# Gate and up products of the feed-forward with the tokens standing still, their product turned by TensorE transposes

## The chip, the core and the metric

One core of one Trainium2 chip runs the kernel. The metric is the device time of one execution in microseconds (us), here the median of three runs. TensorE multiplies a stationary operand of 128 x 128 numbers, which it loads first (the profile's PEld rows), with up to 512 columns that stream past it (the PE rows), and adds the results in PSUM. VectorE (DVE) and ScalarE (ACT) read PSUM and prepare operands; transfers are issued by SyncE (SP).

## The reference, cut to what matters

A decoder trunk of two layers on 256 tokens of width 2048: a layer with dilated attention, then one with latent attention, each followed by a SwiGLU feed-forward of hidden width 5632. All of it is float32.

```python
def swiglu(xn, w_gu, w_down):                      # xn (256, 2048), w_gu (2048, 2 * 5632), w_down (5632, 2048)
    g, u = jnp.split(xn @ w_gu, 2, axis=-1)
    return (jax.nn.silu(g) * u) @ w_down

for layer in range(DEPTH):                         # DEPTH = 2
    ...
    h = h + swiglu(rms_norm(h, ffn_norm_g[layer]), ffn_w_gu[layer], ffn_w_down[layer])
return rms_norm(h, final_norm_g)
```

## The kernel before

**Precision.** Every float32 operand of the large products is split into two float32r parts, hi + lo. A product is made of three: hi by hi, hi by lo, lo by hi. Activations lie transposed, features on partitions: `xT[:, k, 0:256]` holds the hi part of feature tile k for 256 tokens, `xT[:, k, 256:512]` the lo part.

**Weights.** `WeightStream` walks a fixed list of units of 1 MB (2048 float32 per partition). SP loads a unit into one of four `raw` buffers; ACT makes `hi` by two casts (L141), DVE makes `lo` by two subtractions (L142), each half a unit. `hi` and `lo` have three buffers each, so the split of a unit can start when TensorE has finished the unit three before it. The stream has 176 units for gate and up (two layers of 88), each 8 feature tiles by 256 weight columns, and 88 units for the down product, each 4 feature tiles by 512 columns.

**Two forms of product.** `product` takes an accumulator of two PSUM banks (two such accumulators exist), and for each unit calls one of these:

- `w_stationary` (gate, up, and attention's queries and keys): 128 weight columns stand still, the tokens stream. For each feature tile and each of two blocks of 128 weight columns there are two matmuls: the hi weights against 512 columns [hi | lo of the tokens] (L398), and the lo weights against 256 columns (L402). The result has features on partitions, with two halves that are still to be added.
- `x_stationary` (attention's values, the output projection, down): 128 tokens stand still, 512 weight columns stream. For each feature tile and each of two token tiles there are three matmuls of 512 columns (L419, L420, L421). The result has tokens on partitions.

**Feed-forward.** `ffn` works through the 44 hidden tiles of 128 in three parts of 16, 16 and 12. In a part it computes gate and up for two hidden tiles at a time (two units for each): ACT copies one half of the accumulator (L438), DVE adds the halves (L439), DVE multiplies gate by the tokens' rms scale `R` (L389; `across` made R with a small matmul, L383), ACT applies Silu (L604), DVE multiplies gate by up (L606), and `put_split` writes hi and lo of the hidden tiles into `hT` (ACT L326, DVE L327). Then the part's down product runs, four times 512 output columns, with `hT` standing still; `add` puts each result into the residual `h` (L610).

**Transposes.** `transposed` turns token-major tiles into features on partitions: four TensorE transposes of 128 x 128 into a PSUM bank (L351), then `put_split` from the bank. Two banks, eight transposes, are one call for 512 columns. Before the change it serves the normed operands (`h`, `xt`) and the latent vectors (`cc`).

**Order.** Each engine runs its own list in order. `Later` puts a piece of work behind the matmuls of a following unit: `later.put(1, f)` runs f after the matmuls of the next unit, so TensorE has a unit to do while the other engines prepare what f reads.

Of the kernel before, what the change touches and what calls it, by code (L numbers as in the profile page):

```python
# [36 lines left out]
# Weight tiles between a head's projections and its scores, its values.  # L37
# [9 lines left out]
def shape_constants():  # L47
    """Identity, attention masks and rotary tables: functions of the shapes alone."""
    c = np.zeros((P, C_END), np.float32)
    c[:, C_ID:C_ID + P] = np.eye(P, dtype=np.float32)  # L50

    def allowed(q, k, window, dil):
        dist = q - k
        return (dist >= 0) & (dist <= window) & (dist % dil == 0)

    def put(at, blocks):
        m = np.concatenate([allowed(q[:, None], k[None, :], w, d) for q, k, w, d in blocks], axis=1)
        c[:, at:at + m.shape[1]] = np.where(m, np.float32(0.0), np.float32(NEG))

    # Layer A keeps the even tokens in tile 0 and the odd ones in tile 1.  # L60
    i = np.arange(P)
    par = (2 * i, 2 * i + 1)
    order = np.concatenate(par)
    put(C_M0, [(q, order, *A_GROUPS[0]) for q in par])
    put(C_M1, [(q, q, *A_GROUPS[1]) for q in par])
    put(C_M2, [(q, q, *A_GROUPS[2]) for q in par])
    put(C_MB, [(i, i, S, 1), (i + P, np.arange(S), S, 1)])

    def angles(dim):
        f = np.float32(THETA) ** (-np.arange(0, dim, 2, dtype=np.float32) / np.float32(dim))  # L70
        a = np.arange(S, dtype=np.float32)[:, None] * f.astype(np.float32)[None, :]
        return np.cos(a).T.astype(np.float32), np.sin(a).T.astype(np.float32)

    ca, sa = (t[:, order] for t in angles(A_ROT))
    c[:A_ROT, C_CA:C_CA + S] = np.concatenate([ca, ca], axis=0)
    c[:A_ROT, C_SA:C_SA + S] = np.concatenate([-sa, sa], axis=0)
    cb, sb = angles(ROPE)
    c[:, C_CB:C_CB + S] = np.concatenate([cb, cb, cb, cb], axis=0)
    c[:, C_SB:C_SB + S] = np.concatenate([-sb, sb, -sb, sb], axis=0)
    return c  # L80


class WeightStream:
    """Weight tiles in the order of use: loads run ahead, and each float32 tile is split
    exactly into two float32r parts (hi + lo) ahead of the matmuls. form: "dup" writes the
    columns of every k twice, "heads" puts the rotary columns of a pair of heads side by side."""
# [17 lines left out]
    def pieces(self, raw, hi, lo, form, gain):  # L104
        """(source, hi, lo, gain) of every split operation."""
# [7 lines left out]
        elif gain is None:  # L113
            flat = lambda t: t.rearrange("p k c -> p (k c)")  # noqa: E731
            n = nk // 2
            for ks in (slice(0, n), slice(n, nk)):
                yield flat(raw[:, ks]), flat(hi[:, ks]), flat(lo[:, ks]), None
        else:
            for k in range(nk):
                src, dst = raw[:, k, :], [hi[:, k, :], lo[:, k, :]]  # L120
                if form == "dup":
                    src = src.unsqueeze(1).broadcast_to([P, 2, ncol])
                    dst = [t.rearrange("p (o c) -> p o c", o=2) for t in dst]
                yield src, dst[0], dst[1], gain[:, k:k + 1]

    def split(self, upto):
        nc = self.nc
        while self.n_split < min(upto, len(self.units)):
# [8 lines left out]
            view = lambda t: t[:, :nk * ncol].rearrange("p (k c) -> p k c", c=ncol)  # noqa: E731  # L137
# [23 lines left out]
class Later:  # L161
    """Work put behind the matmuls of the following weight tiles, so that TensorE has those to do
    while the other engines prepare its operands."""
# [16 lines left out]
def kernel(ctx, tc, consts, x, attn_norm_g, ffn_norm_g, a_w_qkv, a_w_o, kv_norm_g,  # L180
# [23 lines left out]
    # TensorE's clock rises after some microseconds of work: have it up when the data is here.  # L204
# [10 lines left out]
    def gain_cols(vec, name):  # L215
        """vec [n * P] -> [P, n]: rows of P, to be turned by a transpose."""
# [19 lines left out]
    def load_rest():  # L236
        """The constants and gains that the first products don't need."""
# [41 lines left out]
    def units_ffn(layer):  # L279
        for k0, n in FFN_PARTS:  # L280
            for j in range(k0, k0 + n, 2):
                for base in (0, FF):
                    for k in range(0, KD, 8):
                        add_unit(ffn_w_gu[layer], k, 8, base + j * P, 256)
            for c in range(0, D, 512):
                for k in range(k0, k0 + n, 4):
                    add_unit(ffn_w_down[layer], k, 4, c, 512)
# [28 lines left out]
    con = lambda at, n, rows=P: cst[:rows, at - P:at - P + n]  # noqa: E731  # L316
# [6 lines left out]
    def put_split(dst_hi, dst_lo, src, scale=None):  # L323
        """dst_hi + dst_lo = src (times a value per partition), exactly."""
# [8 lines left out]
    def squares(src, total, on_vector=False):  # L333
        """total [P, 1] = the sum of squares of src [P, n] along the free axis."""
# [9 lines left out]
    def transposed(srcs, dstT, k0, gain):  # L344
        """srcs: [P tokens, n] by token tile -> dstT[:, k0 + j, hi 0:S | lo S:2S], features on partitions."""
# [16 lines left out]
    def rsqrt_mean(ssq, n, dst):  # L362
        """dst = (ssq / n + eps) ** -0.5."""
# [4 lines left out]
    def token_scale(ssq, name):  # L368
        """rms scale by token from partial sums of squares [P, NT, n]."""
# [6 lines left out]
    def across(r, name):  # L376
        """r [P tokens, NT] -> [P, S], the tokens' values along the free axis of every partition."""
# [13 lines left out]
    def w_stationary(acc, hi, lo, xT, k0, first, last, cols):  # L391
        """acc[:, i, :] += (weights' columns cols(i))^T [xT hi | xT lo], lo parts of weights on xT hi."""
        nk = hi.shape[1]
        for kk in range(nk):
            k = k0 + kk
            for i, sl in enumerate(cols):
                st, sp = first and kk == 0, last and kk == nk - 1
                big_mm = lambda: mm(out=acc[:, i, :], lhsT=sl(hi, kk), rhs=xT[:, k, :],  # noqa: B023,E731  # L398
                                    start=st, stop=sp)  # noqa: B023
# [6 lines left out]
    def col(i, n=P):  # L406
        return lambda t, kk: t[:, kk, i * n:(i + 1) * n]

    def x_stationary(acc, hi, lo, xT, k0, first, last, rhs=None, ncol=512, ts=range(NT)):
        """acc[:, t, :] += (tokens of tile t) @ weights."""  # L410
# [12 lines left out]
    def product(stationary, xT, K, **kw):  # L423
        """xT's K feature tiles with the next weight tiles, into a new accumulator."""
# [10 lines left out]
    def halves(acc, n, dst):  # L435
        """dst [P, n, S] = acc[:, :, :S] + acc[:, :, S:]."""
# [4 lines left out]
    def masked(dst, ps, mk, mx):  # L441
        """dst = ps + mk, mx = its maximum by row."""
# [3 lines left out]
    def softmax(parts, m, scale, nscale):  # L446
        """parts[t] [P queries, keys] masked scores, m [P, NT] their maxima -> probabilities."""
        nb = small.tile([P, NT], F32, tag="sm_nb", name="sm_nb")
        if isinstance(scale, float):
            nc.vector.tensor_scalar(out=nb, in0=m, scalar1=nscale, scalar2=None, op0=ALU.mult)  # L450
            by = lambda t: scale  # noqa: E731
        else:
            nc.vector.tensor_tensor(out=nb, in0=m, in1=nscale, op=ALU.mult)
            by = lambda t: scale[:, t:t + 1]  # noqa: E731
# [10 lines left out]
    def keys_first(blocks):  # L465
        """Transposes of [P, P] blocks of probabilities, side by side."""
# [27 lines left out]
    with tc.tile_pool(name="attn_a", bufs=2) as ap:  # L494

        def rope_a(t):
            sw = ap.tile([A_ROT, 2, S], F32, tag="sw", name="sw", bufs=1)
            nc.vector.stream_shuffle(sw, t[:A_ROT], swap)
            bc = lambda r: r.unsqueeze(1).broadcast_to([A_ROT, 2, S])  # noqa: E731
# [22 lines left out]
        def values_a(head, sm, vs):  # L522
# [11 lines left out]
            back = lambda d: d.rearrange("p (i t) -> p t i", t=NT)  # noqa: E731  # L534
# [38 lines left out]
    def out_projection(acc, oT, gain, name):  # L573
        """h += attention output @ w_o (its first columns in acc); the next normed operand,
        still to be scaled by token, and that scale."""
# [12 lines left out]
    def ffn(xT, rstd, finish):  # L588
        """h += swiglu(xT scaled by token); finish(c, t) when a piece of h is complete."""
        row = {}  # L590
        later.put(1, lambda: row.update(R=across(rstd, "R")))
        with tc.tile_pool(name="ffn", bufs=2) as fp:
            for part, (k0, n) in enumerate(FFN_PARTS):
                last = part == len(FFN_PARTS) - 1
                hT = big_tile([P, 16, 2 * S], F32R, "hT")
                for j in range(0, n, 2):
                    gu = []
                    for which in range(2):
                        acc = product(w_stationary, xT, KD, cols=(col(0), col(1)))
                        t = fp.tile([P, 2, S], F32, tag=f"gu{which}", name=f"gu{which}")  # L600
                        halves(acc, 2, t)
                        if which == 0:
                            times_row(t, row["R"], 2)
                            nc.scalar.activation(out=t, in_=t, func=AF.Silu)  # L604
                        gu.append(t)
                    nc.vector.tensor_tensor(out=gu[1], in0=gu[1], in1=gu[0], op=ALU.mult)  # L606
                    put_split(hT[:, j:j + 2, 0:S], hT[:, j:j + 2, S:2 * S], gu[1])

                def add(acc, c, t):
                    nc.vector.scalar_tensor_tensor(out=chunk(t, c), in0=acc[:, t, :], scalar=rstd[:, t:t + 1],  # L610
                                                   in1=chunk(t, c), op0=ALU.mult, op1=ALU.add)
                    if last:  # noqa: B023
                        finish(c, t)

                for c in range(4):
# [4 lines left out]
                    else:  # the very last columns: one token tile after the other  # L620
# [29 lines left out]
    with tc.tile_pool(name="attn_b", bufs=2) as bp:  # L650

        def rope_b(dst, t):
            """dst(rows) = rotary of t [P = 2 x (32 | 32), S]."""
# [8 lines left out]
        def latent(at, gain, lag):  # L662
            """rms_norm(xT @ (gained weights)) into ccT, transposed and gained."""
# [25 lines left out]
        # Rotary queries of one head of a pair each, zero in the other head's rows.  # L689
# [127 lines left out]
```

## Time and profile before

| what | us |
|---|---|
| median of 3 runs (lowest 2730.53, highest 2733.0) | 2730.87 |
| profiled execution, first to last instruction (its span) | 2728.2 |
| TensorE busy in it | 2715.6 |
| VectorE busy | 1612.6 |
| ScalarE busy | 1204.2 |

The profiled execution's own device time is not among the rows of the profile; its span is 2.7 us under the median of the runs. A matmul's row lasts longer than the time to the next matmul, since matmuls overlap in the array: the cost of one in a stream is the distance of two starts, and the cost of a stage is the distance from its first start to the next stage's first start.

### The profile page before, as it was taken

The numbers are of one execution on the slowest core, as the hardware profiler recorded it, in microseconds if no ns is written. First come the engines' busy times: TensorE is split into PE (matmuls) and PEld (weight loads), VectorE is DVE, ScalarE is ACT, GpSimd is POOL, SyncE is SP. The second block draws the span as 40 slices with busy tenths as digits, with TensorE's granted clock in tenths as the row PEclk, the third lists the DMA queues.
The fourth block names the chain that finished last, engine by engine and source line by source line (L and its number), as shares of the span: only waits on it lengthen the run. The fifth ranks groups of instructions, "written<-read, shape, count | busy, mean of one in ns | idle before, by whom it ended". The sixth has DMA issues, their size and how long they took to land.

```text
span 2728.2 us, 34772 instructions
## 1 busy us (share of the span) xinstructions
PE 2715.6 (100%) x14398; PEld 2323.1 (85%) x14398; DVE 1612.6 (59%) x2240; ACT 1204.2 (44%) x1605; POOL 5.5 (0%) x12
## 2 busy tenths in 40 slices
PE   9999999999999999999999999999999999999998
PEld 7888888888888888888888888888888888888887
DVE  5666576576477555545555555587555555555554
ACT  5344444443434444434443444555444434443443
POOL 0000000000000000000000000000000000000000
PEclk9999999999999999999999999999999999999999
DMA  7545555554554555555555555454555555555553
GB/s 282 182 162 171 181 171 170 185 182 161 182 175 166 201 181 188 187 190 194 188 185 187 185 187 196 140 156 145 174 181 186 194 190 187 187 190 192 185 201 124
DMA packets 389870, 495.91 MB, mean 182 GB/s; under 512 B 9848, under 2 KB 293200, under 8 KB 389200
## 3 DMA queue, kind: packets, MB, share of 16 engines
q1 hardware_dynamic: 389088, 492.63, 54.2%
q8 instruction: 113, 1.85, 0.3%
q10 hardware_dynamic: 624, 1.07, 0.1%
q14 instruction: 45, 0.37, 0.0%
HBM read 491.57 MB, written 2.10 MB: 181 GB/s over the span
## 4 chain that ended last, share of the span: by engine, by line
PE 98%; DVE 0%; issue 0%; ACT 0%; DMA 0%; SPq 0%; POOL 0%; POOLq 0%; DVEq 0%; ACTq 0%
PE acc L398 39%; PE acc L402 20%; PE acc L420 12%; PE acc L421 12%; PE acc L419 12%; PE bank L513 1%; PE bank L470 1%; PE bank L528 1%; PE bank L351 1%; PE bank L532 1%; PE bank L705 0%; PE bank L704 0%; PE bank L715 0%; DMA xt<-in_x_dram 0%; DVE lo L142 0%
## 5 line engine op out<-in xcount | busy, mean ns | idle before, releaser
L142 DVE TENSOR_TENSOR lo<-raw,hi 128x1024 fp32r<-128x1024 f32 (+2 forms) x930 | 1082.4, 1193 | 570.4 <-ACT hi L141 570.1
L141 ACT CAST hi<-raw 128x1024 fp32r<-128x1024 f32 (+2 forms) x930 | 912.7, 1030 | 859.7 <-issue 358.8
L398 PE MATMUL acc<-xT_f,hi 128*128 128x512 f32 x2816 | 987.6, 398 | 0.0
L402 PE MATMUL acc<-xT_f,lo 128*128 128x256 f32 x2816 | 776.9, 281 | 0.0
L398 PEld LDWEIGHTS acc<-xT_f,hi 128*128 128x128 f32 x2816 | 523.8, 188 | 122.7
L398 PE MATMUL acc<-xT_a,hi 128*128 128x512 f32 x1536 | 544.2, 399 | 0.0
L402 PEld LDWEIGHTS acc<-xT_f,lo 128*128 128x128 f32 x2816 | 531.8, 189 | 7.8
L402 PE MATMUL acc<-xT_a,lo 128*128 128x256 f32 x1536 | 423.7, 281 | 0.0
L398 PEld LDWEIGHTS acc<-xT_a,hi 128*128 128x128 f32 x1536 | 286.8, 188 | 63.5
L438 ACT COPY t<-acc 128x512 f32<-128x512 f32 x161 | 92.7, 576 | 502.8 <-PE acc L398 502.8
L402 PEld LDWEIGHTS acc<-xT_a,lo 128*128 128x128 f32 x1536 | 289.5, 188 | 3.7
L419 PE MATMUL acc<-hi,hT 128*128 128x512 f32 x704 | 274.1, 389 | 0.0
L421 PE MATMUL acc<-hi,hT 128*128 128x512 f32 x704 | 273.9, 389 | 0.0
L420 PE MATMUL acc<-lo,hT 128*128 128x512 f32 x704 | 273.9, 389 | 0.0
L439 DVE TENSOR_TENSOR gu<-acc,t 128x512 f32<-128x512 f32 x88 | 60.9, 692 | 244.2 <-ACT t L438 244.2
L421 PEld LDWEIGHTS acc<-hi,hT 128*128 128x128 f32 x704 | 132.1, 188 | 27.5
L420 PEld LDWEIGHTS acc<-lo,hT 128*128 128x128 f32 x704 | 132.1, 188 | 27.3
L419 PEld LDWEIGHTS acc<-hi,hT 128*128 128x128 f32 x704 | 132.2, 188 | 27.2
L420 PE MATMUL acc<-lo,xT_a 128*128 128x512 f32 x384 | 150.3, 391 | 0.8 <-DVE lo L142 0.8
L421 PE MATMUL acc<-hi,xT_a 128*128 128x512 f32 x384 | 151.0, 393 | 0.0
L419 PE MATMUL acc<-hi,xT_a 128*128 128x512 f32 x384 | 150.9, 393 | 0.0
L420 PEld LDWEIGHTS acc<-lo,xT_a 128*128 128x128 f32 x384 | 72.3, 188 | 16.1 <-DVE lo L142 1.5
(169 smaller groups left out, 2080.7 us busy)
## 6 DMA issues: line engine op xcount, KB each, us to landing
raw<-in_ffn_w_gu_dram SPq DMA_DIRECT2D x176, 1024.0 KB, 4.9
raw<-in_a_w_qkv_dram SPq DMA_DIRECT2D x143, 1024.0 KB, 4.9
raw<-in_ffn_w_down_dram SPq DMA_DIRECT2D x88, 1024.0 KB, 4.9
raw<-in_a_w_o_dram SPq DMA_DIRECT2D x16, 1024.0 KB, 4.9
raw<-in_b_w_o_dram SPq DMA_DIRECT2D x16, 1024.0 KB, 4.9
raw<-in_b_w_kv_b_dram SPq DMA_DIRECT2D x8, 1024.0 KB, 5.4
raw<-in_b_w_q_b_dram SPq DMA_DIRECT2D x8, 768.0 KB, 4.6
raw<-in_b_w_q_a_dram SPq DMA_DIRECT2D x4, 1024.0 KB, 5.0
```

The lines of the kernel that those rows point to most:

```text
L141: nc.scalar.copy(out=h, in_=src)
L142: nc.vector.tensor_tensor(out=l, in0=src, in1=h.bitcast(F32), op=ALU.subtract)
L351: nc.tensor.transpose(out=ps[:, jj * S + t * P:jj * S + (t + 1) * P], in_=srcs[t][:, (j + jj) * P:(j + jj + 1) * P], identity=ident)
L398: big_mm = lambda: mm(out=acc[:, i, :], lhsT=sl(hi, kk), rhs=xT[:, k, :], # noqa: B023,E731 start=st, stop=sp) # noqa: B023
L402: mm(out=acc[:, i, 0:S], lhsT=sl(lo, kk), rhs=xT[:, k, 0:S], start=False, stop=False)
L419: mm(out=acc[:, t, :ncol], lhsT=xh, rhs=rhs(hi, kk), start=st, stop=False)
L420: mm(out=acc[:, t, :ncol], lhsT=xh, rhs=rhs(lo, kk), start=False, stop=False)
L421: mm(out=acc[:, t, :ncol], lhsT=xl, rhs=rhs(hi, kk), start=False, stop=sp)
L438: nc.scalar.copy(out=t1[:, :n, :], in_=acc[:, :n, S:2 * S])
L439: nc.vector.tensor_tensor(out=dst, in0=acc[:, :n, 0:S], in1=t1[:, :n, :], op=ALU.add)
L470: nc.tensor.transpose(out=ps[:, i * P:(i + 1) * P], in_=b, identity=ident)
L513: mm(out=ps[:, t * n:(t + 1) * n], lhsT=q[:, hh, qt], rhs=kt[:, hh, ks], start=True, stop=True)
```

## The change

Gate and up use `x_stationary` instead of `w_stationary`. A step is now four hidden tiles (512 columns) instead of two, and a unit of gate and up is 4 feature tiles by 512 columns instead of 8 by 256, of the same 1 MB. ACT applies Silu straight from the accumulator, with the tokens' rms scale as a value per partition, into a new tile `hid` (tokens on partitions); DVE multiplies `hid` by the up accumulator; after the next unit's matmuls `transposed` turns `hid` by eight TensorE transposes and splits it into `hT`. The sum of the halves, the row `R` and its small matmul are gone from the feed-forward. Comments and docstrings were removed as well.

```diff
     def units_ffn(layer):
         for k0, n in FFN_PARTS:
-            for j in range(k0, k0 + n, 2):
+            for j in range(k0, k0 + n, 4):
                 for base in (0, FF):
-                    for k in range(0, KD, 8):
-                        add_unit(ffn_w_gu[layer], k, 8, base + j * P, 256)
+                    for k in range(0, KD, 4):
+                        add_unit(ffn_w_gu[layer], k, 4, base + j * P, 512)
...
     def ffn(xT, rstd, finish):
-        row = {}
-        later.put(1, lambda: row.update(R=across(rstd, "R")))
-        with tc.tile_pool(name="ffn", bufs=2) as fp:
+        with tc.tile_pool(name="ffn", bufs=3) as fp:
             for part, (k0, n) in enumerate(FFN_PARTS):
                 last = part == len(FFN_PARTS) - 1
                 hT = big_tile([P, 16, 2 * S], F32R, "hT")
-                for j in range(0, n, 2):
-                    gu = []
-                    for which in range(2):
-                        acc = product(w_stationary, xT, KD, cols=(col(0), col(1)))
-                        t = fp.tile([P, 2, S], F32, tag=f"gu{which}", name=f"gu{which}")
-                        halves(acc, 2, t)
-                        if which == 0:
-                            times_row(t, row["R"], 2)
-                            nc.scalar.activation(out=t, in_=t, func=AF.Silu)
-                        gu.append(t)
-                    nc.vector.tensor_tensor(out=gu[1], in0=gu[1], in1=gu[0], op=ALU.mult)
-                    put_split(hT[:, j:j + 2, 0:S], hT[:, j:j + 2, S:2 * S], gu[1])
+                for j in range(0, n, 4):
+                    hid = fp.tile([P, NT, 512], F32, tag="hid", name="hid")
+                    acc = product(x_stationary, xT, KD)
+                    for t in range(NT):
+                        nc.scalar.activation(out=hid[:, t, :], in_=acc[:, t, :], func=AF.Silu,
+                                             scale=rstd[:, t:t + 1])
+                    acc = product(x_stationary, xT, KD)
+                    nc.vector.tensor_tensor(out=hid, in0=acc, in1=hid, op=ALU.mult)
+                    later.put(1, lambda j=j, hid=hid, hT=hT:
+                              transposed([hid[:, t, :] for t in range(NT)], hT, j, None))
```

On TensorE, at the start of the first feed-forward (xT_f is its normed operand, h the residual), the order before has pairs of a long and a short matmul, with the transposes of the last piece of h and the matmul for R between them:

```order
4705 L402 MATMUL acc<-xT_f_7145,lo 128x256
4706 L398 MATMUL acc<-xT_f_7145,hi 128x512
4707 L351 MATMUL bank<-ident,h 128x128 x8
4708 L383 MATMUL bank<-diag,ones 128x256
4709 L402 MATMUL acc<-xT_f_7145,lo 128x256
```

On TensorE, after the first unit of the second step, the order of the changed kernel has triples of 512 columns, and the eight transposes of the first step's hid between two of them:

```order
4892 L421 MATMUL acc<-hi,xT_f_7145 128x512
4893 L351 MATMUL bank<-ident,hid 128x128 x8
4894 L419 MATMUL acc<-hi,xT_f_7145 128x512
4895 L420 MATMUL acc<-lo,xT_f_7145 128x512
4896 L421 MATMUL acc<-hi,xT_f_7145 128x512
```

Such a group of eight stands once in each step of four hidden tiles, 22 times in all, always after the 24 matmuls of the unit that follows the step; the group for h stays where it was and the matmul for R is gone.

On VectorE, at the start of a part of the feed-forward before (lo is a half unit of split weights, gu the gate or up tile, t the copied half), one step of two hidden tiles reads:

```order
911 L142 TENSOR_TENSOR lo<-raw,hi 128x1024 x4
912 L439 TENSOR_TENSOR gu_11574<-acc,t_11575 128x512
913 L389 TENSOR_TENSOR gu_11574<-gu_11574,R 128x512
914 L142 TENSOR_TENSOR lo<-raw,hi 128x1024 x4
915 L439 TENSOR_TENSOR gu_11661<-acc,t_11662 128x512
916 L606 TENSOR_TENSOR gu_11661<-gu_11661,gu_11574 128x512
917 L142 TENSOR_TENSOR lo<-raw,hi 128x1024
918 L327 TENSOR_TENSOR hT<-gu_11661,hT 128x2x256
```

On VectorE, at the start of a part in the changed kernel, one step of four hidden tiles reads:

```order
1199 L142 TENSOR_TENSOR lo<-raw,hi 128x1024 x16
1200 L601 TENSOR_TENSOR hid<-acc,hid 128x1024
1201 L142 TENSOR_TENSOR lo<-raw,hi 128x1024 x3
1202 L327 TENSOR_TENSOR hT<-bank,hT 128x2x256 x2
1203 L142 TENSOR_TENSOR lo<-raw,hi 128x1024 x13
```

Three operations that stood between the halves of weights are gone, the multiplication stands alone and waits for the up product, and the writing of hT has moved three half units behind it, where it waits for the transposes and for ACT's casts of them.

## Rows read from the trace of the kernel before

**Rows 1.** The page: the span, the busy times of the engines, and TensorE's granted clock in 40 slices in tenths of full speed.

```profile
span 2728.2 us, 34772 instructions
...
PE 2715.6 (100%) x14398; PEld 2323.1 (85%) x14398; DVE 1612.6 (59%) x2240; ACT 1204.2 (44%) x1605; POOL 5.5 (0%) x12
...
PEclk9999999999999999999999999999999999999999
```

**Rows 2.** The page: the chain of work that ended last, by engine and by line.

```profile
PE 98%; DVE 0%; issue 0%; ACT 0%; DMA 0%; SPq 0%; POOL 0%; POOLq 0%; DVEq 0%; ACTq 0%
PE acc L398 39%; PE acc L402 20%; PE acc L420 12%; PE acc L421 12%; PE acc L419 12%; PE bank L513 1%; PE bank L470 1%; PE bank L528 1%; PE bank L351 1%; PE bank L532 1%; PE bank L705 0%; PE bank L704 0%; PE bank L715 0%; DMA xt<-in_x_dram 0%; DVE lo L142 0%
```

**Rows 3.** Busy time in the six gate and up stages, of the instructions that read or write xT_f alone. Columns: the stretch, its length, then for PE, PEld, DVE and ACT the busy time (and instructions), the granted clock, the DMA engines' busy share, GB/s. The first three stages are layer 0's, the sum is over all six.

```profile
979.90:1161.79 181.89, 180.93 (x1024) 156.83 (x1023) 1.74 (x4) 1.70 (x4) 1.00 0.56 185
1248.83:1429.42 180.59, 180.59 (x1024) 156.77 (x1023) 0.00 (x0) 0.00 (x0) 1.00 0.57 187
1516.46:1651.90 135.44, 135.44 (x768) 117.54 (x767) 0.00 (x0) 0.00 (x0) 1.00 0.56 186
...
sum 995.84, PE 993.92 PEld 862.30 DVE 3.48 ACT 3.40; mean PE 165.65 PEld 143.72 DVE 0.58 ACT 0.57
```

**Rows 4.** The same view of two of the down stages, of the instructions that read or write hT alone. The second is layer 0's last; it holds three groups of eight transposes of h.

```profile
1161.79:1248.83 87.04, 87.04 (x384) 71.88 (x383) 0.68 (x1) 0.62 (x1) 1.00 0.58 194
...
1651.90:1719.90 68.00, 66.11 (x288) 53.65 (x287) 0.68 (x1) 0.62 (x1) 1.00 0.56 186
```

**Rows 5.** TensorE's instructions in order of time where a down stage ends and a gate and up stage begins: start, length, line, operation.

```profile
1248.15 0.39 PE L419 MATMUL acc<-hi,hT 128*128 128x512 f32 x1
1248.38 0.39 PE L420 MATMUL acc<-lo,hT 128*128 128x512 f32 x1
1248.60 0.39 PE L421 MATMUL acc<-hi,hT 128*128 128x512 f32 x1
1248.83 0.39 PE L398 MATMUL acc<-xT_f,hi 128*128 128x512 f32 x1
1249.06 0.28 PE L402 MATMUL acc<-xT_f,lo 128*128 128x256 f32 x1
1249.17 0.40 PE L398 MATMUL acc<-xT_f,hi 128*128 128x512 f32 x1
```

**Rows 6.** The chain that ended last in order of time (start, length, what), its transposes in layer 0's last down stage. Three units of the down product lie from one group to the next.

```profile
1673.82 0.87 PE bank L351 x8
1691.05 0.87 PE bank L351 x8
1708.28 0.87 PE bank L351 x8
```

**Rows 7.** TensorE's instructions in order of time around the first of these groups.

```profile
1673.43 0.39 PE L421 MATMUL acc<-hi,hT 128*128 128x512 f32 x1
1673.66 1.03 PE L351 MATMUL bank<-ident,h 128*128 128x128 f32 x8
1674.45 0.48 PE L419 MATMUL acc<-hi,hT 128*128 128x512 f32 x1
1674.76 0.39 PE L420 MATMUL acc<-lo,hT 128*128 128x512 f32 x1
```

**Rows 8.** The groups of instructions by line and shape: the transposes of h. After the bar: busy time, mean ns of one, idle time before them.

```profile
L351 PE MATMUL bank<-ident,h 128*128 128x128 f32 x96 | 12.4, 272 | 0.0
```

**Rows 9.** The same view: the halves of the weights' split; then the operations that the change removes or that are like those which it adds, on VectorE and ScalarE.

```profile
L142 DVE TENSOR_TENSOR lo<-raw,hi 128x1024 fp32r<-128x1024 f32 x894 | 1062.8, 1218 | 570.4 <-ACT hi L141 570.1
L141 ACT CAST hi<-raw 128x1024 fp32r<-128x1024 f32 x894 | 896.2, 1050 | 854.8 <-issue 358.8 <-PE acc L421 319.6 <-PE acc L398 173.7
...
L439 DVE TENSOR_TENSOR gu<-acc,t 128x512 f32<-128x512 f32 x88 | 60.9, 692 | 244.2 <-ACT t L438 244.2
...
L604 ACT ACTIVATE gu<-gu 128x512 f32<-128x512 f32 x44 | 27.6, 626 | 0.0
...
L544 ACT ACTIVATE v<-acc,rstd 128x512 f32<-128x512 f32 x24 | 15.2, 685 | 42.1 <-PE acc L421 42.1
...
L582 DVE TENSOR_TENSOR h<-acc,h 128x1024 f32<-128x1024 f32 x8 | 9.8, 1225 | 15.8 <-PE acc L421 13.7 <-DMA h<-in_x_dram 2.1
...
L327 DVE TENSOR_TENSOR xT_b<-bank,xT_b 128x512 fp32r<-128x512 f32 x8 | 5.1, 682 | 0.0
...
L326 ACT CAST xT_b<-bank 128x512 fp32r<-128x512 f32 x8 | 4.2, 582 | 0.0
```

**Rows 10.** VectorE's instructions in order of time in a down stage, around the end of one product (in brackets: idle time before, and what ended it).

```profile
1205.51 1.41 DVE L610 SCALAR_TENSOR_TENSOR h<-acc,rstd,h 128x512 f32<-128x512 f32 x2 [2.00 <-PE acc L421]
1206.84 2.35 DVE L142 TENSOR_TENSOR lo<-raw,hi 128x1024 fp32r<-128x1024 f32 x2
1212.03 2.36 DVE L142 TENSOR_TENSOR lo<-raw,hi 128x1024 fp32r<-128x1024 f32 x2 [2.84 <-ACT hi L141]
```

**Rows 11.** The page: DMA issues of the weights of gate and up (8 runs of 1 KB on each partition) and of down (4 runs of 2 KB): count, KB each, us from issue to landing.

```profile
raw<-in_ffn_w_gu_dram SPq DMA_DIRECT2D x176, 1024.0 KB, 4.9
...
raw<-in_ffn_w_down_dram SPq DMA_DIRECT2D x88, 1024.0 KB, 4.9
```

**Rows 12.** TensorE's instructions in order of time at a group of transposes of the latent vectors whose operand came late.

```profile
1769.28 0.44 PE L351 MATMUL bank<-ident,cc 128*128 128x128 f32 x2 [0.51 <-ACT cc L675]
```

## Prediction

> **What bounds the kernel now.** I read the page's busy times and the chain first: TensorE is busy for 2715.6 of 2728.2 us at a granted clock of 1.00, that is at its 2.4 GHz level, and 98% of the chain that ended last is TensorE [rows 1, 2]. No other engine is near: VectorE 59%, ScalarE 44%. So the time moves by what TensorE's own stream gains or loses, and by nothing else unless a new wait appears in it. Next I read the stages that the change touches. The six gate and up stages last 995.84 us together, with 1024 or 768 matmuls on a clock of 1.00; within them TensorE waits only at the start [rows 3]. The down stages show the other form of product, which the change puts in place of the present one [rows 4].
>
> **The price of a unit in the two forms.** A unit is 1 MB of weights in both. With the weights standing still it is 16 pairs, 32 matmuls: the second stage has 32 units in 180.59 us, 5.643 us each, 0.353 us a pair; the third has 24 units in 135.44 us, the same 5.643 [rows 3]. With the tokens standing still it is 4 feature tiles x 2 token tiles x 3 = 24 matmuls of 512 columns: 384 matmuls, 16 units, take 87.04 us, which is 5.440 us a unit and 0.2267 us a matmul [rows 4]; the starts 1248.15, 1248.38, 1248.60 show it directly [rows 5]. The columns streamed are the same, 16 x (512 + 256) = 24 x 512 = 12288. What differs is only how many matmuls they are cut into, and how a short one's weight load fits behind it. So the gain is small: 0.203 us in 5.643, under 4%, where a glance at the rows' durations (0.398 + 0.281 against 3 x 0.389) would promise 14%. Those durations overlap; the distances of the starts don't.
>
> **Sum, part by part.**
> 1. Gate and up: 176 units x 5.440 = 957.44 us. Of what stands in the present stages beside units, the two groups that transpose the last piece of h stay; they cost 2 x 0.907 = 1.81 (next point). So 995.84 becomes 959.25: 36.59 us less. This counts the small matmul for R and its surroundings, too: the first stage is 181.89 - 180.59 = 1.30 us longer than the second, 0.91 of it the transposes of h, 0.39 the matmul for R and what waited there, twice 0.8 us [rows 3].
> 2. The transposes: 22 groups of eight. Layer 0's last down stage has 12 units and three such groups in 68.00 us; 12 x 5.440 = 65.28, so a group costs 2.72 / 3 = 0.907 us [rows 4]. The chain says the same: from 1673.82 to 1691.05 and to 1708.28 it is 17.23 us, against 3 x 5.440 = 16.32 [rows 6]. These are transposes of float32 tiles of the same shape among the same matmuls, so I take 0.907: 22 x 0.907 = 19.95 us more. The bounds are the group's length on the chain, 0.87, and its length in order of time, 1.03 [rows 6, 7]: 19.1 to 22.7 us.
> 3. Net: 36.59 - 19.95 = 16.6 us less.
>
> A rule of the Trainium skill speaks against point 2. Page "TensorE: Matmul & The Clock Gate", Part 4 (PE-mode transpose), gives about 275 ns for a 128 x 128 transpose in one kernel's context; 176 of them would be an estimated 48.4 us, more than the whole gain, and the kernel would come out near 2743. This trace has that number, 272 ns, as the mean length of a transpose's row, yet eight of them take 0.87 us on the chain [rows 6, 8]: the price in a stream is the distance, 0.11 us.
>
> **What has to stay hidden.** Per step of four hidden tiles the other engines get less work, not more: ACT has two Silu from PSUM (like the 685 ns activation from an accumulator) and two casts from a bank (582 ns), DVE one multiplication of 1024 columns (like the 1225 ns one) and two subtractions (682 ns); four additions of halves (692 ns), two Silu (626 ns) and others go [rows 9]. That relief is worth nothing by itself, since TensorE is the bound. Three chains could turn into a wait:
> - *hid before its transposes.* The multiplication is queued behind the halves of weights of a unit that was split before, and the transposes come after one more unit, 5.44 us. In a down stage DVE picks up a finished accumulator at once, after 2.00 us of idleness [rows 10], so hid is there after 1.3 to 1.5 us: about 4 us to spare.
> - *hT before the down product reads it.* The last step's four tiles are read by the third unit (parts of 12) of down, at 2 x 5.44 + 0.91 = 11.8 us; the transposes begin at 5.44. ACT has one half cast in front (1.05), then two casts (1.16), and DVE finishes 0.7 to 1.4 us later: near 9.1 us, 2.7 to spare [rows 9]. In parts of 16 it is a unit more.
> - *Weights.* The split of a unit takes ACT 2.1 and DVE 2.4 us [rows 9] and has two units' time. The Silu pair in front of it adds 1.4, the hT casts 1.2. The loads land in 4.9 us for either shape of run [rows 11], four buffers ahead, and down stages already run at this pace with 194 GB/s [rows 4]. Here, and for the two PSUM accumulators (each free long before the 21.8 us product that reuses it begins), I take zero.
>
> **The rivals.**
> - *A, hid comes late.* If DVE or ACT were behind, TensorE would stop at each of the 22 groups. The one late group in the trace lost 0.51 us, waiting for ACT's cc [rows 12]: 22 x 0.51 = 11.2, and the kernel would be at 2725.5, hardly faster. For it: hid passes through two engines whose lists hold weight work. Against: 4 us of room.
> - *B, slower: each transpose costs its row.* If transposes of hid did not overlap with each other and with the matmuls' loads, each would take 0.272 us [rows 8], 22 x 8 x 0.272 = 47.9 us, and 2730.87 - 36.59 + 47.9 = 2742.2. It decides from 36.59 / 176 = 0.208 us a transpose. Against: 0.113 at the groups measured [rows 4].
> - *C, slower: gate and up gain nothing.* If the stage went by columns alone, or by the arrival of weights at 187 GB/s [rows 3], a unit would stay at 5.643, only 0.8 us would be saved and 20 paid: about 2750. Against: the down stages' 5.440 with the same loads, splits and operand layout [rows 4].
>
> Rival C can also be read in the Trainium skill: the page "TensorE: Matmul & The Clock Gate", section "Back-to-back issue gap", puts a lone matmul's gap at N / 2.4 + 2.5 ns; by it a unit would be an estimated 5.20 us before and 5.18 after, the saving 4 us and the kernel near 2746. The distances measured here, 0.353 a pair and 0.227 a matmul, are both above it and not equally so, which is where the gain lies [rows 3, 4].
>
> **How the numbers follow.** The sum is made on the profiled execution: 2728.2 - 16.6 = 2711.6 us of span. The runs' median lies 2.7 above that span, and nothing outside the stages changes, so 2730.87 - 16.6 = 2714.2. With the bounds of point 2 it is 2713.4 to 2717.0, and the three runs scatter by 2.5 us. Chances: the forecast 0.84, A 0.08, B 0.03, C 0.03; 0.02 for something unseen. The range is 2711 to 2721: the forecast with its bounds and the scatter, stretched towards a partial A (0.3 us lost at each group gives 2720.8). No change is within 0.2% (5.5 us, about what a measurement of this kernel can tell): 2725.4 to 2736.3. A lies on that edge. Faster 0.89, same 0.06, slower 0.05.
>
> **What would show it.** In the changed profile: gate and up stages of 32 units near 174.1 us plus 0.91 for each group in them, matmul starts 0.227 apart, PE rows of L398 and L402 on xT_f gone, 176 transposes of hid with some 20 us on the chain, no idle time before them, a granted clock of 1.00 throughout. Idle time before L351 released by hid would be A; a group much longer than 0.91 would be B; a unit above 5.5 us, C. The forecast is wrong if the triples on xT_f don't keep the pace of those on hT, or if TensorE waits for lo or hT anywhere in these stages.

## The result, and the profile after

| | before | changed |
|---|---|---|
| median of 5 runs, us (lowest to highest) | 2731.51 (2730.53 to 2733.0) | 2713.31 (2712.54 to 2714.91) |
| span of the profiled execution, us | 2728.2 | 2711.5 |

The ratio is 0.9934, with a 95% interval of 0.9922 to 0.9947: 18.2 us faster by the medians, 16.7 by the spans. The forecast was 2714.2 and 2711.6 of span. That the span agrees to 0.1 us is in part luck, since the spans of the five executions run from 2710.8 to 2713.1; what repeats more closely is the length of the stages below.

The page of the changed kernel, as [rows 1]:

```profile
span 2711.5 us, 31961 instructions
...
PE 2698.2 (100%) x13162; PEld 2269.7 (84%) x13162; DVE 1521.5 (56%) x2080; ACT 1162.8 (43%) x1517; POOL 5.5 (0%) x12
...
PEclk9999999999999999999999999999999999999999
```

Its chain by engine and by line, as [rows 2]:

```profile
PE 98%; DVE 0%; issue 0%; ACT 0%; DMA 0%; SPq 0%; POOL 0%; POOLq 0%; DVEq 0%; ACTq 0%
PE acc L420 24%; PE acc L421 24%; PE acc L419 24%; PE acc L398 15%; PE acc L402 7%; PE bank L351 1%; PE bank L513 1%; PE bank L470 1%; PE bank L528 1%; PE bank L532 1%; PE bank L701 0%; PE bank L700 0%; PE bank L711 0%; DMA xt<-in_x_dram 0%; DVE lo L142 0%
```

TensorE is as full as before, in a shorter span. VectorE and ScalarE are relieved of 91 and 41 us of busy time; whether that has a part in the difference is tested below. The gate and up stages, instructions on xT_f alone, as [rows 3]; the first three are layer 0's, the sum is over six:

```profile
979.81:1157.52 177.71, 175.19 (x768) 143.67 (x767) 1.74 (x4) 1.70 (x4) 1.00 0.58 189
1245.47:1422.27 176.80, 174.91 (x768) 143.74 (x767) 0.00 (x0) 0.00 (x0) 1.00 0.58 190
1510.21:1642.59 132.38, 131.12 (x576) 107.78 (x575) 0.00 (x0) 0.00 (x0) 1.00 0.59 191
...
sum 973.78, PE 962.45 PEld 790.36 DVE 3.48 ACT 3.40; mean PE 160.41 PEld 131.73 DVE 0.58 ACT 0.57
```

and the two down stages of [rows 4]:

```profile
1157.52:1245.47 87.95, 87.32 (x384) 71.81 (x383) 1.28 (x2) 1.07 (x2) 1.00 0.60 192
1642.59:1711.49 68.90, 66.39 (x288) 53.58 (x287) 1.28 (x2) 1.07 (x2) 1.00 0.55 184
```

The second gate and up stage holds 32 units and three groups of transposes: 176.80 - 3 x 0.907 = 174.08, 5.440 us a unit. The fourth group of the part stands in the down stage, which is 0.91 us longer than before. Layer 0's whole feed-forward, from its first matmul to the next layer's first (979.81 to 1711.49), takes 731.68 us where it took 740.00 (979.90 to 1719.90): 8.32 us less, and the second layer's loses as much: 16.64 in all. The starts at the border, as [rows 5], show one pace on both sides of it:

```profile
1245.24 0.39 PE L421 MATMUL acc<-hi,hT 128*128 128x512 f32 x1
1245.47 0.39 PE L419 MATMUL acc<-hi,xT_f 128*128 128x512 f32 x1
1245.69 0.39 PE L420 MATMUL acc<-lo,xT_f 128*128 128x512 f32 x1
```

The chain in order of time, its transposes of hid, as [rows 6]: 44.42 and 44.43 us apart, which is 8 units (43.52) and 0.90.

```profile
1029.85 0.87 PE bank L351 x8
1074.27 0.87 PE bank L351 x8
1118.70 0.87 PE bank L351 x8
```

The new groups of instructions, as [rows 8, 9]:

```profile
L327 DVE TENSOR_TENSOR hT<-bank,hT 128x512 fp32r<-128x512 f32 x44 | 28.2, 682 | 0.0
L598 ACT ACTIVATE hid<-acc,rstd 128x512 f32<-128x512 f32 x44 | 27.9, 686 | 68.7 <-PE acc L421 68.7
L601 DVE TENSOR_TENSOR hid<-acc,hid 128x1024 f32<-128x1024 f32 x22 | 26.9, 1224 | 43.9 <-PE acc L421 43.9
L326 ACT CAST hT<-bank 128x512 fp32r<-128x512 f32 x44 | 23.5, 587 | 0.0
L351 PE MATMUL bank<-ident,hid 128*128 128x128 f32 x176 | 22.8, 272 | 0.0
```

The transposes (L351) have no idle time ahead of them. VectorE in order of time at the tightest place, the start of layer 0's last down stage (up ended at 1642.59), to be read beside [rows 10]:

```profile
1642.79 1.23 DVE L601 TENSOR_TENSOR hid<-acc,hid 128x1024 f32<-128x1024 f32 x1 [1.99 <-PE acc L421]
...
1650.62 1.28 DVE L327 TENSOR_TENSOR hT<-bank,hT 128x512 fp32r<-128x512 f32 x2
```

So hid is there 1.4 us after the end of up and hT 9.3 us after it; TensorE needs them at 5.4 and 11.8.

### The profile page after: what moved, and what is told of

Same layout as the page of the kernel before. It is cut to its first block, busy times and chain, and to the rows that moved or that the text cites. A ratio compares the mean times of both kernels' runs of the same rounds, so it can differ in the third digit from the quotient of the medians.

```text
span 2711.5 us, 31961 instructions
## 1 busy us (share of the span) xinstructions
PE 2698.2 (100%) x13162; PEld 2269.7 (84%) x13162; DVE 1521.5 (56%) x2080; ACT 1162.8 (43%) x1517; POOL 5.5 (0%) x12
## 4 chain that ended last, share of the span: by engine, by line
PE 98%; DVE 0%; issue 0%; ACT 0%; DMA 0%; SPq 0%; POOL 0%; POOLq 0%; DVEq 0%; ACTq 0%
PE acc L420 24%; PE acc L421 24%; PE acc L419 24%; PE acc L398 15%; PE acc L402 7%; PE bank L351 1%; PE bank L513 1%; PE bank L470 1%; PE bank L528 1%; PE bank L532 1%; PE bank L701 0%; PE bank L700 0%; PE bank L711 0%; DMA xt<-in_x_dram 0%; DVE lo L142 0%
## 5 line engine op out<-in xcount | busy, mean ns | idle before, releaser
L419 PE MATMUL acc<-hi,xT_f 128*128 128x512 f32 x1408 | 549.3, 390 | 0.0
L421 PE MATMUL acc<-hi,xT_f 128*128 128x512 f32 x1408 | 548.0, 389 | 0.0
L420 PE MATMUL acc<-lo,xT_f 128*128 128x512 f32 x1408 | 547.9, 389 | 0.0
L421 PEld LDWEIGHTS acc<-hi,xT_f 128*128 128x128 f32 x1408 | 264.3, 188 | 55.0
L420 PEld LDWEIGHTS acc<-lo,xT_f 128*128 128x128 f32 x1408 | 264.3, 188 | 54.4
L419 PEld LDWEIGHTS acc<-hi,xT_f 128*128 128x128 f32 x1408 | 264.3, 188 | 54.3
L438 ACT COPY t<-acc 128x512 f32<-128x512 f32 (+1 forms) x73 | 41.0, 561 | 185.7 <-PE acc L398 185.7
```

Source lines behind the costliest of these rows:

```text
L419: mm(out=acc[:, t, :ncol], lhsT=xh, rhs=rhs(hi, kk), start=st, stop=False)
L420: mm(out=acc[:, t, :ncol], lhsT=xh, rhs=rhs(lo, kk), start=False, stop=False)
L421: mm(out=acc[:, t, :ncol], lhsT=xl, rhs=rhs(hi, kk), start=False, stop=sp)
L438: nc.scalar.copy(out=t1[:, :n, :], in_=acc[:, :n, S:2 * S])
```

## The experiments

Since the sum came out, the question was whether its terms are the reasons or only happen to add up. Each time below stands against runs of the kernel before on the same chip (medians of 2729.82 to 2732.62 us). The changed kernel is 18.2 us faster than its own, and what a run gains or loses to it is taken from these two differences.

**Is 0.907 us what a group costs?** Once the transposes were left out, so that hT is split from hid as it lies:

```diff
-                              transposed([hid[:, t, :] for t in range(NT)], hT, j, None))
+                        for i in range(0, 4, 2):
+                            put_split(hT[:, j + i:j + i + 2, 0:S], ..., hid[:, :, i * P:(i + 2) * P])
```

Once each was made twice, in `transposed`, which gets `times=2` for hid:

```diff
-            for jj in range(2):
+            for jj in [0, 1] * times:
```

> The changed kernel without its 176 transposes of hid: hT is split from hid as it lies, so the hidden tiles are not turned (that part of the computation is left out). Theory T (TensorE's stream alone sets the time, a group of eight transposes costs 0.907 us): 2713.3 - 22 x 0.907 = 2693.4 us. Rival R (each transpose costs its row of 0.272 us, and gate and up gained correspondingly more): 2713.3 - 47.9 = 2665. Rival S (the gain came from lighter VectorE and ScalarE work and longer DMA runs, and TensorE has slack): no change, 2713.

Measured: 2692.37 against 2729.82, 37.5 us faster than before, 19.3 more than the changed kernel. The second gate and up stage, instructions on xT_f, is now 32 units and nothing else: 32 x 5.440 us.

```profile
1240.27:1414.36 174.09, 174.09 (x768) 143.96 (x767) 0.00 (x0) 0.00 (x0) 1.00 0.59 193
```

> The changed kernel with every transpose of hid made twice into the same bank. Theory T: eight more at 0.109 us in a group, without a second entry into and exit from the stream: 22 x 0.872 = 19.2 us more, 2732.5. Rival R: 47.9 more, 2761. Rival S: 2713.

Measured: 2732.14 against 2729.82, ratio 1.0008 (0.9998 to 1.0018): 20.5 us above the changed kernel, the whole gain given back. TensorE in order of time at the first group: 1.66 us from its start to the next matmul, where eight had 0.79.

```profile
1028.36 1.91 PE L351 MATMUL bank<-ident,hid 128*128 128x128 f32 x16
1030.02 0.48 PE L419 MATMUL acc<-hi,xT_f 128*128 128x512 f32 x1
```

Both fit T; R (2665 and 2761) and S fall. The traces are closer than the medians: layer 0's feed-forward, 731.68 us in the changed kernel, takes 721.70 without its 11 groups (978.25 to 1699.95) and 741.28 with them doubled (978.49 to 1719.77). That is 0.907 us less and 0.873 us more for each group, as T had it.

**Did lighter engines or longer DMA runs help?**

```diff
+                    side(acc)      # for gate and up: twice (ACT copy, DVE add, DVE multiply) of 512 columns
-                self.nc.sync.dma_start(out=v, in_=ap)
+                for c in (slice(0, 256), slice(256, 512)):
+                    self.nc.sync.dma_start(out=v[:, :, c], in_=ap[:, :, c])
```

> The changed kernel with the weights of gate and up loaded in runs of 1 KB again (two DMAs of 256 columns for a unit) and with extra work that nobody reads on ScalarE and VectorE in each step: four copies of 512 columns from the accumulators, four additions and four multiplications, about what the change had removed or more. Theory T: none of it is on the path, 2713.3 within 1.5 us. Rival S: the gain goes back, 2722 to 2731.

Measured: 2712.34 against 2729.82, ratio 0.9935 (0.992 to 0.995), as the changed kernel. Its second gate and up stage, all instructions (PE, PEld, DVE, ACT busy), has 101.09 us of VectorE and 78.87 of ScalarE, where the kernel before has 100.5 and 79.1, and it takes the same 176.80 us.

```profile
1245.49:1422.29 176.80, 176.80 (x793) 146.62 (x792) 101.09 (x103) 78.87 (x92) 0.00 (x0) 1.00 0.61 190
```

The lighter load is still worth something as room. VectorE and TensorE in order of time at the first group: with the extra work in front of it, hid is ready only 0.33 us before its transposes start, where the changed kernel has 4.0 us.

```profile
1028.16 1.22 DVE L614 TENSOR_TENSOR hid<-acc,hid 128x1024 f32<-128x1024 f32 x1
1029.71 1.03 PE L355 MATMUL bank<-ident,hid 128*128 128x128 f32 x8
```

**What does the unit between up and the transposes hide?**

```diff
-                    later.put(1, lambda j=j, hid=hid, hT=hT:
-                              transposed([hid[:, t, :] for t in range(NT)], hT, j, None))
+                    transposed([hid[:, t, :] for t in range(NT)], hT, j, None)
```

> The changed kernel with the transposes of hid right behind the up product instead of one unit later. Theory T: TensorE waits in each of the 22 groups for VectorE's multiplication, 0.2 us until it starts, 1.22 for it and some 0.1 for the signal, 1.5 us each, 33 us in all: 2746 (2742 to 2750). If the unit between were needless: 2713.

Measured: 2712.23 against 2729.82; no loss. The expectation missed, since the kernel that ran did not have the order that was written: the scheduler that lays out the lists had put seven matmuls of the next product ahead of the transposes. VectorE's multiplication, and TensorE in order of time from the seventh of them on:

```profile
1023.60 1.23 DVE L601 TENSOR_TENSOR hid<-acc,hid 128x1024 f32<-128x1024 f32 x1 [2.00 <-PE acc L421]
1024.76 0.39 PE L419 MATMUL acc<-hi,xT_f 128*128 128x512 f32 x1
1024.99 1.03 PE L351 MATMUL bank<-ident,hid 128*128 128x128 f32 x8
```

Seven matmuls are 1.6 us, a little more than hid takes: it is ready at 1024.83, 0.16 us before its transposes start. So the run said that 1.6 us of cover suffice, not that none is needed. The next one held the order:

```diff
+                    last_turn = transposed([hid[:, t, :] for t in range(NT)], hT, j, None)
...
+                    with tc.issue_after(last_turn.ins):      # the next product's matmuls queue behind it
                         acc = product(x_stationary, xT, KD)
```

> As the run without a unit between the up product and the transposes, but with TensorE's list held to that order: the transposes of hid stand directly behind the last matmul of up, and the next product behind them. Theory T: TensorE waits at 22 places for VectorE, 0.2 us until it starts, 1.22 for the multiplication, less than 0.1 for the signal; 1.5 us each, 33 in all: 2746 (2742 to 2750), with idle time before L352 put down to hid. If cover is worth nothing: 2713.

Measured: 2746.07 against 2730.11, ratio 1.006 (1.0045 to 1.0075): 34 us above the changed kernel and 16 slower than the kernel before. TensorE's wait for hid (in all, times, longest), and TensorE in order of time at the first of these places:

```profile
PE bank L352 <- DVE hid L604: 29.0, 22, 1.3
...
1025.01 0.39 PE L423 MATMUL acc<-hi,xT_f 128*128 128x512 f32 x1
1026.72 1.09 PE L352 MATMUL bank<-ident,hid 128*128 128x128 f32 x8 [1.32 <-DVE hid L604]
```

The wait is counted from the end of the last matmul's row. By starts it is 1.71 us from that matmul to the transposes, where 0.23 is usual, so 1.5 us are lost at each of 22 places, as expected. So rival A is a real mechanism; the cover turns it off.

**Who wins: the standing tokens, or the 512 columns?**

```diff
-                        add_unit(ffn_w_gu[layer], k, 4, base + j * P, 512)
+                        add_unit(ffn_w_gu[layer], k, 8, base + j * P, 256)
...
-                    acc = product(x_stationary, xT, KD)
+                    acc = product(x_stationary, xT, KD, ncol=256)
```

> The changed kernel with the old cut of the weights: units of 8 feature tiles by 256 columns, steps of two hidden tiles, tokens still standing still, so a unit is 48 matmuls of 256 columns in place of 24 of 512, and the transposes come in 44 groups of four. Theory T (a matmul costs its columns at 2.4 GHz plus some 13 ns, as the 512 columns in 0.2267 us say; 256 columns: 0.120): a unit 5.76 us, 176 x 0.32 = 56 us more and 1 for the groups, 2770, slower than before. If only columns counted: 2714. If each matmul had to wait for its own weight load (0.188 us a row): 9.0 us a unit, 3340. If it is the standing tokens as such that win: near 2713.

Measured: 2769.91 against 2730.11, ratio 1.0146 (1.0129 to 1.0163). Standing tokens with short matmuls lose 40 us to the kernel before. So it isn't the standing tokens as such that win. Its second gate and up stage, TensorE in order of time in the first one, and two groups of instructions of the kernel:

```profile
1255.31:1442.66 187.35, 186.00 (x1536) 184.68 (x1535) 0.00 (x0) 0.00 (x0) 1.00 0.55 181
...
1002.00 0.28 PE L419 MATMUL acc<-hi,xT_f 128*128 128x256 f32 x1
1002.12 0.28 PE L420 MATMUL acc<-lo,xT_f 128*128 128x256 f32 x1
```

```profile
L419 PE MATMUL acc<-hi,xT_f 128*128 128x256 f32 x2816 | 799.9, 284 | 0.0
...
L419 PEld LDWEIGHTS acc<-hi,xT_f 128*128 128x128 f32 x2816 | 540.6, 192 | 0.2
```

Loads whose rows last 0.192 us follow one another every 0.12 us, so the rows overlap and their length doesn't set the pace. The 256 columns that a long matmul has more cost 0.2267 - 0.120 = 0.107 us, their time at 2.4 GHz, and either length leaves 13 ns above its columns.

**Why does a pair cost 0.353 and not 0.2267 + 0.120 = 0.347?** The products left with standing weights got another order, in the changed kernel: both long matmuls of a feature tile, then both short ones (short ones first in a product's last feature tile).

```diff
-                if st: big_mm()
-                mm(out=acc[:, i, 0:S], lhsT=sl(lo, kk), ...)
-                if not st: big_mm()
+            for form in ("short", "long") if sp and not st else ("long", "short"):
+                for i, sl in enumerate(cols): ...      # one matmul of this form
```

> The changed kernel with another order in the product that is left in the old form (queries and keys of the first layer, 1536 pairs, and 160 in the second): for each feature tile both matmuls of 512 columns, then both of 256, in place of long and short in turn. A pair costs 0.353 us in the trace, where 0.2267 + 0.120 of the other form would be 0.347. Theory L (the long one pays for a weight load that the short one ahead of it cannot hide): every second long one gets 0.009 us back, 848 x 0.009 = 7.6 us, 2705.7, and the version beats both. Theory M (a long matmul with the weights standing still is 0.236 us whatever stands before it, as the starts of the few long ones in a row say): within 1.5 us of 2713.3.

Measured: 2709.43 against 2731.38, ratio 0.992 (0.9906 to 0.9933): 22.0 us faster than before, 3.7 more than the changed kernel. Neither theory has it: L wanted 7.6, M nothing. Both took 0.353 us, the price of a pair in gate and up, for the price of these pairs; in the changed kernel's trace the median distance from a long one to the next start is 0.232 us and from a short one 0.117, 0.349 a pair.

> The kernel before, with the same new order of long and short matmuls in the form with standing weights (4512 pairs instead of the 1696 that the change leaves). Theory T: the new order saves per pair what it saved in the run before (2.5 us of span, 3.9 us by the medians, in 1696 pairs: 0.0015 to 0.0023 us each), 6.7 to 10.4 us here: 2721 to 2725, so that it brings in about half of what the change brings, without any transposes, and the tokens standing still stay ahead. If the gate and up pairs gain the whole distance to 0.347 us: 4512 x 0.006 = 27 us, 2704, and the old form is the better one.

Measured: 2716.81 against 2731.7, ratio 0.9945 (0.9929 to 0.9962). The order alone brings the kernel before 14.9 us, more than expected: the expectation had taken the queries' and keys' saving for gate and up, where a pair goes from 0.353 to 0.349. Its second gate and up stage has 5.583 us a unit:

```profile
1244.85:1423.50 178.65, 178.65 (x1024) 155.79 (x1023) 0.00 (x0) 0.00 (x0) 1.00 0.58 189
```

Next, all long matmuls of a unit and then all short ones (`todo = longs + shorts`, the other way round in a product's last unit), beside a repeat:

> The changed kernel, its queries and keys with all long matmuls of a unit of weights first and all short ones behind them (or the other way round in a unit that ends a product). Theory D (what a pair pays over 0.347 us comes at the changes from long to short and back: 0.353 with a change after each matmul, 0.350 with one after every second): nearly no changes are left, 0.347 a pair, 1536 x 0.006 = 9 us against the changed kernel, 2704. Theory M (a long matmul with standing weights costs some 0.233 whatever its neighbours): as the run with two and two, 2708 to 2711.

> The two and two order once more, on the same chip as the run beside it, for a direct comparison: 2709.4 within 1.5 us by either theory.

Measured: 2708.79 and 2709.05 against 2731.68, ratios 0.9917 (0.9904 to 0.9931) and 0.9918: no difference between the two here; against the changed kernel 9 us were expected and 4.7 came. The 9 us went wrong by the same premise: sorted by unit, these medians are 0.227 and 0.120, so a pair had 0.002 us to gain and not 0.006, some 3 us in 1536. In the kernel before, the same order:

> The kernel before, with all long matmuls of a unit together and all short ones together in every product with standing weights, gate and up among them. Theory D (a pair is 0.2267 + 0.120 where no long and short ones alternate): gate and up 16 x 0.347 = 5.55 us a unit, a stage of 32 units 177.6, together 16 to 17 us less, and the 4.6 us that queries and keys gained in the run of the changed kernel: 2710 to 2711; the old form is then within 2 us of the changed kernel with the same order (2708.8), and the change's gain is the cure of a price that the order has as well. If gate and up stay at 5.58 us as with two and two: 2716 to 2717, and standing tokens keep a lead of 8 us.

Measured: 2711.5 against 2732.62, ratio 0.9924 (0.9908 to 0.9941), 21.1 us faster. Its second gate and up stage takes 5.557 us a unit, as D said, with no idle time. TensorE in order of time in it shows runs of 32, since the short ones that end a product's first unit meet those that begin its last:

```profile
1241.57:1419.38 177.81, 177.81 (x1024) 157.30 (x1023) 0.00 (x0) 0.00 (x0) 1.00 0.58 191
...
1300.76 4.00 PE L404 MATMUL acc<-xT_f,lo 128*128 128x256 f32 x32
```

## Why the prediction was right

- **Gate and up at 5.440 us a unit**: measured 5.440, with the transposes and (in the first experiment) without them. Rival C falls.
- **A group of transposes at 0.907 us**: so it is in both kinds of stage, and leaving them out or doubling them moved the time by 19.3 and 20.5 us where 19.95 and 19.2 were due; by the trace of layer 0's feed-forward it is 0.907 and 0.873 a group, as was due. Rival B, 0.272 a transpose, falls.
- **Net 16.6 us**: the stages give it, twice the 8.32 us of layer 0's feed-forward; by the medians it is 18.2, within the scatter of the runs.
- **Nothing new waits**: hid and hT came at 1.4 and 9.3 us, where 1.3 to 1.5 and 9.1 were worked out; no wait of TensorE for them. Rival A did not come. Where its cover was taken away it cost 34 us, three times the 11.2 at which the prediction had priced it from a wait of another kind.
- **The reason given for the unit's price holds in part.** The two prices were measured, not derived, and so the sum holds whatever their reason. The step said that only the number of matmuls differs, and how a short one's weight load fits. In a stream of one length a matmul costs its columns at 2.4 GHz and 13 ns more, at 512 columns (0.2267) and at 256 (0.120) alike: 8 matmuls fewer in a unit are 0.107 of the 0.203 us. The other 0.096 is 16 times 0.006 for long and short in turn, and that goes nearly away when like ones stand together (5.557 a unit). That it is the short one's weight load is not shown; where all matmuls are short, the loads keep up with one start in 0.12 us.
- So the change won little more than an order of the old form wins as well. With that order the old form comes out at 0.9924 of the kernel before, with no transposes; the changed kernel is at 0.9934, and at 0.9917 with the better order in its remaining pairs, the fastest complete version run here. Between 0.9917 and 0.9924 the intervals leave no verdict. In the traces layer 0's feed-forward is 732.41 us in the old form with that order (975.37 to 1707.78) and 731.68 in the changed kernel: the order alone brings 7.59 of the 8.32 us.

What stays open is what on TensorE makes alternating lengths dearer. One rival is not separated: with long and short in turn the two matmuls of a pair write the same PSUM bank, while in both new orders the bank changes at every matmul, so the step from 5.643 to 5.583 us a unit may be in part the banks'. The step from 5.583 to 5.557 is not, and with the tokens standing still three matmuls in a row write one bank at 0.2267 us each. Open is also why a pair in turn is cheaper in the queries and keys (0.349 by the medians) than in gate and up (0.236 + 0.118 = 0.354). Other work interrupts them; where nothing does, 16 pairs of the changed kernel from 300.20 to 305.84 take the 0.353 of gate and up.

## What to carry to other kernels

Where TensorE is full, price a rewrite by the distance of starts in the stage that it copies, never by the length of rows: lengths promised 14% here, starts 3.6%, and the starts were right to the hundredth of a microsecond. Before turning a product round, try its order: matmuls of equal length side by side gave the old form's feed-forward 7.6 us a layer where the new form gave 8.3, without a transpose. Take a price from the very stage that it is used for: 0.353 us a pair, right in gate and up, was wrong in the queries and keys. And read the order that a scheduler really made before an experiment on order is believed.

## What the runs showed of the hardware that was not expected

In gate and up, a stream that alternates 512 and 256 columns with standing weights costs 0.353 us a pair; the same matmuls in runs of 32 cost 0.347 (5.557 us in 16 pairs), and two and two 0.349 (5.583). Weight loads whose rows last 0.192 us sustained one start in 0.12 us: PEld was busy for 184.68 of 187.35 us, and still a matmul of 256 columns took no more above its columns (13 ns) than one of 512 columns did.
